# Output stores of a tiled einsum on two DMA queues, each issued behind the copies of the next tile

## Chip, cores and metric

One core of one Trainium2 chip. The metric is the device time of one launch in microseconds (us), lower is better.

## The reference

```python
def setup_inputs():
    batch, n_heads, seq_t, seq_s, channels = 8, 12, 512, 512, 64
    # x, y: (8, 12, 512, 64) float32

def reference(x, y):
    return np.einsum('bhtc,bhsc->bhts', x, y).astype(np.float32)
```

Two inputs of 12.6 MB each, one output of 100.7 MB: per head a 512 x 64 by 64 x 512 product. There is little arithmetic per byte written.

## The kernel before

The inputs are loaded in 12 groups of 8 heads (x and y, 1 MB each), cast to bf16 and rearranged, then transposed on VectorE. The output is made in 48 tiles of 128 partitions x 4096 float32 (2 MB): eight matmuls into PSUM, two copies of 1536 columns by ScalarE, one of 1024 by VectorE, and one store. Inputs and output tiles share five slots of 2 MB in SBUF.

```python
    SLOTS = 5
    # ... (views, constants cut)
    slots = ctx.enter_context(tc.tile_pool(name="slots", bufs=SLOTS))
    # ... (other pools cut)
    def slot():
        return slots.tile([P, K * S], fp32, name="slot")

    def load(g):
        both = slot()
        nc.sync.dma_start(both[:, :R * C], xv[g])
        nc.sync.dma_start(both[:, R * C:], yv[g])
        loaded[g] = both
    # ... (compress, mix, transposes cut: the input work)
    def result(o):

        i, h = divmod(o, 2)
        xT, yT = made[i]
        otf = slot()
        ot = otf.rearrange("p (r s) -> p r s", s=S)
        for k, n in ((0, 3), (3, 3), (6, 2)):
            pm = (pm3pool if n == 3 else pm2pool).tile([P, n, S], fp32, name=f"pm{n}")
            for j in range(n):
                nc.tensor.matmul(
                    pm[:, j, :], xT[:, k + j, h, :], yT[:, h * S:(h + 1) * S], start=True, stop=True
                )
            copy(nc.scalar if n == 3 else nc.vector, ot[:, k:k + n, :], pm)
        if h == 0 and i + 2 < 2 * NG:
            transposes(i + 2)
        elif h == 1 and FIRST <= i + 4 < 2 * NG:
            mix(i + 4, behind)
        return lambda: nc.sync.dma_start(ov[i, h], otf)

    with tc.manual_schedule():
        for g in range(SLOTS):
            load(g)
        # ... (memsets cut)
        stores = []
        for g in range(NG):
            compress(g)
            mix(g // 2, [nc.gpsimd] * 4, (g % 2,))
            if g in (2, 4):
                transposes(g // 2 - 1)
            if g < 5:
                load(g + SLOTS)
            elif g in (5, 7, 9):
                stores.append(result(len(stores)))
            elif g in (6, 8):
                load(g // 2 + 7)
        for store in stores:
            store()
        for o in range(len(stores), 4 * NG):
            result(o)()
```

The schedule is by hand: each engine executes its instructions in the order in which the program emits them.

Of the kernel before, what the change touches and what calls it, by code (L numbers as in the profile page):

```python
# [1 line left out]

# [4 lines left out]


@with_exitstack
def kernel(  # L10
    ctx: ExitStack,
    tc: tile.TileContext,
    x: bass.AP,
    y: bass.AP,
    out: bass.AP,
):










    nc = tc.nc
    B, H, T, C = x.shape
    _, _, S, _ = y.shape
    P = 128  # L30
    G = 8
    Q = P // G
    R = T // Q
    NG = B * H // G
    K = 8
    E = R // K
    D = 32
    SLOTS = 5
    fp32 = mybir.dt.float32
    bf16 = mybir.dt.bfloat16  # L40
    u32 = mybir.dt.uint32
    COPY = mybir.ActivationFunctionType.Copy
    assert C == 2 * D and S == T and R == D and Q * 2 == D

    xv = x.rearrange("b h t c -> (b h t c)").rearrange("(g p n) -> g p n", p=P, n=R * C)
    yv = y.rearrange("b h t c -> (b h t c)").rearrange("(g p n) -> g p n", p=P, n=R * C)
    ov = out.rearrange("b h t s -> (b h t s)").rearrange(
        "(o u h q n) -> o h q u n", u=2, h=2, q=Q * E, n=K * S
    )

    const = ctx.enter_context(tc.tile_pool(name="const", bufs=1))
    kept = ctx.enter_context(tc.tile_pool(name="kept", bufs=NG))
    slots = ctx.enter_context(tc.tile_pool(name="slots", bufs=SLOTS))
    tpool = ctx.enter_context(tc.tile_pool(name="tpool", bufs=3))
    pm3pool = ctx.enter_context(tc.tile_pool(name="pm3psum", bufs=2, space=bass.MemoryType.PSUM))
    pm2pool = ctx.enter_context(tc.tile_pool(name="pm2psum", bufs=1, space=bass.MemoryType.PSUM))

    loaded, inputs, mixed, made = {}, {}, {}, {}
    zeroed = [const.tile([P, K * E * D], u32, name=f"xb{half}") for half in range(2)]
    in_front = [nc.vector, nc.gpsimd, nc.vector, nc.scalar]  # L60
    behind = [nc.vector, nc.gpsimd, nc.scalar, nc.vector]
    FIRST = NG // 2

    def copy(engine, dst, src):
        if engine is nc.scalar:
            nc.scalar.activation(dst, src, COPY)  # L66
        else:
            engine.tensor_copy(dst, src)  # L68
# [10 lines that stand above are left out]
    def compress(g):  # L79

        both = loaded.pop(g)
        xk = kept.tile([P, R, C], bf16)
        nc.scalar.activation(xk.rearrange("p r c -> p (r c)"), both[:, :R * C], COPY)  # L83
        inputs[g] = xk
        ys = both[:, R * C:].rearrange("p (r c) -> p r c", c=C)
        for half in range(2):
            yb = kept.tile([P, R // 2 * D], u32, name=f"yb{half}")
            yv2 = yb.bitcast(bf16).rearrange("p (j c w) -> p j w c", j=R // 2, w=2)
            for ch in range(2):
                copy(  # L90
                    in_front[2 * half + ch],
                    yv2[ch * 64:(ch + 1) * 64],
                    ys[half * 64:(half + 1) * 64, :, ch * D:(ch + 1) * D].rearrange(
                        "p (j w) c -> p j w c", w=2
                    ),
                )
            mixed[2 * g + half] = yb

    def mix(i, engines, halves=(0, 1)):

        g, half = divmod(i, 2)
        xk = inputs[g]
        xv2 = zeroed[half].bitcast(bf16).rearrange("p (k e c u) -> p k e c u", k=K, e=E, u=2)
        for ch in halves:
            for u in range(2):
                lo = half * 64 + u * D
                copy(
                    engines[2 * ch + u],
                    xv2[(2 * ch + u) * D:(2 * ch + u + 1) * D, :, :, :, u],
                    xk[lo:lo + D, :, ch * D:(ch + 1) * D].rearrange("p (e k) c -> p k e c", k=K),  # L110
                )

    def transposes(i):
        xb, yb = zeroed[i % 2], mixed.pop(i)
        xT = tpool.tile([P, K * D * E], u32)
        nc.vector.transpose(  # L116
            xT.rearrange("p (k r e) -> p k e r", k=K, e=E),
            xb.rearrange("p (k e c) -> p k e c", k=K, e=E),
        )
        yT = tpool.tile([P, D * R // 2], u32)  # L120
        nc.vector.transpose(  # L121
            yT.rearrange("p (r j) -> p j r", r=D), yb.rearrange("p (j c) -> p j c", c=D)
        )
        made[i] = (xT.bitcast(bf16).rearrange("p (k h m) -> p k h m", k=K, h=2), yT.bitcast(bf16))
# [15 lines that stand above are left out]
            transposes(i + 2)  # L140
        elif h == 1 and FIRST <= i + 4 < 2 * NG:
            mix(i + 4, behind)
        return lambda: nc.sync.dma_start(ov[i, h], otf)  # L143

    with tc.manual_schedule():
        for g in range(SLOTS):
            load(g)
        nc.vector.memset(zeroed[0], 0.0)  # L148
        nc.gpsimd.memset(zeroed[1], 0.0)  # L149
# [9 lines that stand above are left out]
                stores.append(result(len(stores)))  # L159
            elif g in (6, 8):  # L160
                load(g // 2 + 7)
        for store in stores:
            store()
        for o in range(len(stores), 4 * NG):
            result(o)()


# [1 line left out]
_INS = ['x', 'y']  # L169
_OUTS = [((8, 12, 512, 512), 'float32')]  # L170


# [23 lines left out]
```

## Time and profile before

| | before |
|---|---|
| time, median of the first 3 runs | 301.96 us (301.9 to 302.25) |
| span of the profiled run | 300.5 us |
| DMA engines, share of the span | 98.7% on one queue |
| busiest compute engine | ScalarE, 66% |
| moved | 125.83 MB (read 25.17, written 100.66) |
| one store, issue to landing, median | 21.7 us |

The lines of the profile are shown in the prediction below. In a line of a stretch, the columns are the stretch, its length, busy time and instructions of PE, PEld (weight loads), DVE (VectorE), ACT (ScalarE) and POOL, then the granted TensorE clock, the mean busy share of the 16 DMA engines, and GB/s. A packet is counted in the stretch in which it starts, so a share can come out a little over 1. A packet is one entry of the trace's DMA table: in the kernel before 6144 of 16 KB (one row of a store's tile), 3072 of 8 KB (one row of a load) and 1152 of 4 bytes. Ring is used here as another word for queue. In a line of waits they are who waited, for what, us in all, times, and the longest.

### The profile page before, as it was taken

How to read it: one execution, taken by the hardware profiler on the slowest of the kernel's cores; microseconds unless marked ns; L12 is line 12 of the kernel's file. 1: busy time of each engine (PE TensorE's matmuls, PEld its weight loads, DVE VectorE, ACT ScalarE, POOL GpSimd, SP SyncE). 2: the span in 40 equal slices, each digit the busy share in tenths (PEclk: the TensorE clock that was granted, in tenths of full speed). 3: DMA queues.
4: the chain of work that ended last, by engine and by line, in shares of the span. 5: the costliest groups of instructions: out<-in, count | busy, mean ns of one | idle time of the engine just before them, and what ended most of it. 6: DMA issues, size and time to landing. Idle time of an engine off the chain costs nothing.

```text
span 300.5 us, 1448 instructions
## 1 busy us (share of the span) xinstructions
PE 148.4 (49%) x384; PEld 47.6 (16%) x384; DVE 189.2 (63%) x157; ACT 198.1 (66%) x139; POOL 82.0 (27%) x59
## 2 busy tenths in 40 slices
PE   0004044228647573765675567666476767475000
PEld 0001011003212121221121122212121222121000
DVE  1568998895997669666767576757765775313000
ACT  4666598999976867686668676777677664647000
POOL 1899989991211011101110111011101100000000
PEclk9999575577997659567756855756955765955555
DMA  7999999999999999999999999999999999999994
GB/s 282 429 424 421 423 422 422 423 435 434 423 434 426 425 438 430 425 443 421 433 436 425 432 430 425 438 430 423 442 423 430 441 421 430 432 422 427 436 425 181
DMA packets 10377, 125.93 MB, mean 419 GB/s; under 512 B 1152, under 2 KB 1152, under 8 KB 1152
## 3 DMA queue, kind: packets, MB, share of 16 engines
q1 hardware_dynamic: 10368, 125.83, 98.7%
q8 instruction: 3, 0.05, 0.1%
q14 instruction: 6, 0.05, 0.0%
HBM read 25.17 MB, written 100.66 MB: 419 GB/s over the span
## 4 chain that ended last, share of the span: by engine, by line
DMA 65%; ACT 15%; DVE 7%; PE 3%; issue 1%; ACTq 1%; SPq 0%; DVEq 0%
DMA out_dram<-slot 56%; ACT slot L66 11%; DMA slot<-in_y_dram 9%; DVE yb L68 4%; PE pm L135 3%; ACT xk L83 3%; DVE xT L116 2%; ACT yb L66 2%; DVE slot L68 1%; DVE yT L121 1%; ACTq L191 0%; SPq L75 0%; ACTq L66 0%; DVEq L68 0%; SPq L143 0%
## 5 line engine op out<-in xcount | busy, mean ns | idle before, releaser
L135 PE MATMUL pm<-yT,xT 128*128 128x512 bf16 x384 | 148.4, 537 | 127.3 <-ACT slot L66 102.2
L66 ACT ACTIVATE slot<-pm 128x1536 f32<-128x1536 f32 x96 | 133.9, 1448 | 65.8 <-DMA out_dram<-slot 51.3
L68 DVE COPY slot<-pm 128x1024 f32<-128x1024 f32 x48 | 58.8, 1225 | 72.0 <-PE pm L135 54.4
L68 POOL COPY xb<-xk 32x1024 bf16<-32x1024 bf16 x42 | 62.2, 1482 | 145.4 <-DVE xT L116 144.3
L135 PEld LDWEIGHTS <-xT 128*128 128x128 bf16 x384 | 47.6, 124 | 227.2 <-issue 193.9
L116 DVE STREAM_TRANSPOSE xT<-xb 128x1024 uint32<-128x1024 uint32 x24 | 49.3, 2054 | 0.7
L68 DVE CAST yb<-slot 64x1024 bf16<-64x1024 f32 x24 | 35.2, 1466 | 13.5 <-DMA slot<-in_y_dram 13.2
L83 ACT ACTIVATE xk<-slot 128x2048 bf16<-128x2048 f32 x12 | 22.9, 1910 | 9.6 <-DMA slot<-in_x_dram 9.4
L68 DVE COPY xb<-xk 32x1024 bf16<-32x1024 bf16 x36 | 26.3, 731 | 0.5
L121 DVE STREAM_TRANSPOSE yT<-yb 128x512 uint32<-128x512 uint32 x24 | 25.0, 1041 | 0.0
L66 ACT ACTIVATE xb<-xk 32x1024 bf16<-32x1024 bf16 x18 | 24.1, 1338 | 0.4
L68 POOL CAST yb<-slot 64x1024 bf16<-64x1024 f32 x12 | 18.8, 1567 | 8.1 <-DMA slot<-in_y_dram 7.4
L66 ACT ACTIVATE yb<-slot 64x1024 bf16<-64x1024 f32 x12 | 15.9, 1324 | 3.6 <-DMA slot<-in_y_dram 3.4
L83 ACT ACT_TABLE_LOAD x1 | 1.3, 1283 | 0.7 <-PEq L180 0.7
L148 DVE MEMSET xb<- 128x1024 uint32 x1 | 0.9, 912 | 1.0 <-PEq L180 1.0
L149 POOL MEMSET xb<- 128x1024 uint32 x1 | 1.0, 952 | 0.3 <-POOLq L180 0.3
L180 POOL MEMSET const-float32-0.0<- 128x1 f32 x1 | 0.1, 98 | 0.2 <-issue 0.2
L180 POOL MEMSET const-float32-1.0<- 128x1 f32 x1 | 0.1, 98 | 0.0
L180 POOL MEMSET const-bfloat16-1.0<- 128x1 bf16 x1 | 0.1, 98 | 0.0
L180 POOL MEMSET const-uint8-127<- 128x1 uint8 x1 | 0.1, 98 | 0.0
## 6 DMA issues: line engine op xcount, KB each, us to landing
out_dram<-slot SPq DMA_DIRECT2D x48, 2048.0 KB, 21.7
slot<-in_x_dram SPq DMA_DIRECT2D x12, 1024.0 KB, 17.5
slot<-in_y_dram SPq DMA_DIRECT2D x12, 1024.0 KB, 19.3
```

Source lines behind the costliest of these rows:

```text
L66: nc.scalar.activation(dst, src, COPY)
L68: engine.tensor_copy(dst, src)
L83: nc.scalar.activation(xk.rearrange("p r c -> p (r c)"), both[:, :R * C], COPY)
L116: nc.vector.transpose(xT.rearrange("p (k r e) -> p k e r", k=K, e=E), xb.rearrange("p (k e c) -> p k e c", k=K, e=E),)
L121: nc.vector.transpose(yT.rearrange("p (r j) -> p j r", r=D), yb.rearrange("p (j c) -> p j c", c=D))
L135: nc.tensor.matmul(pm[:, j, :], xT[:, k + j, h, :], yT[:, h * S:(h + 1) * S], start=True, stop=True)
L148: nc.vector.memset(zeroed[0], 0.0)
L149: nc.gpsimd.memset(zeroed[1], 0.0)
L180: nc = _bacc.Bacc("TRN2", target_bir_lowering=False, num_devices=1)
```

## The change

Half of the stores move to ScalarE's DMA queue, and each store is emitted only after the copies of the next tile. The intent is to have two queues feeding the DMA engines, without making ScalarE wait for VectorE's share of a tile before it may start on the next: by the time ScalarE comes to a store, the tile has long been complete.

```diff
-        return lambda: nc.sync.dma_start(ov[i, h], otf)
+        return lambda: (nc.scalar if h else nc.sync).dma_start(ov[i, h], otf)
...
-        for store in stores:
-            store()
-        for o in range(len(stores), 4 * NG):
-            result(o)()
+        done = len(stores)
+        while len(stores) > 1:
+            stores.pop(0)()
+        for o in range(done, 4 * NG):
+            stores.append(result(o))
+            stores.pop(0)()
+        stores.pop()()
```

## The prediction

A mark in a recorded text stands for a passage that is cut because no trace or run of this case shows it. In the prediction these are rules on how queues share the DMA engines, a ceiling for the rate with what rival B would gain by it in full, and a reason for rival C. The sum came to 301.9 us: the terms that stand give 302.0, and a term of -0.1 us is cut. The lower end of the range, 299.5 us, and "B nearly whole" rested on a cut ceiling for the rate, which wasn't shown.

> **What bounds the kernel now.** I read the page first: the share of each engine, the slices, then the queues.
>
> ```profile
> PE 148.4 (49%) x384; PEld 47.6 (16%) x384; DVE 189.2 (63%) x157; ACT 198.1 (66%) x139; POOL 82.0 (27%) x59
> ...
> DMA  7999999999999999999999999999999999999994
> GB/s 282 429 424 421 423 422 422 423 435 434 423 434 426 425 438 430 425 443 421 433 436 425 432 430 425 438 430 423 442 423 430 441 421 430 432 422 427 436 425 181
> ...
> q1 hardware_dynamic: 10368, 125.83, 98.7%
> HBM read 25.17 MB, written 100.66 MB: 419 GB/s over the span
> ```
>
> No compute engine is busy for more than 66% of the span. The 16 DMA engines are busy for 98.7% of it on the one queue in use, and every slice but the first and the last is full. So the time is 125.83 MB at the rate at which the engines take packets, plus the two ends: 1.3% of 300.5 us is 3.9 us for start and tail together. Next I asked for stretches, in case one hides a hole.
>
> ```profile
> 0.00:54.10 54.10, 10.44 (x24) 3.37 (x25) 38.93 (x29) 36.84 (x24) 44.69 (x33) 0.82 0.98 404
> 54.10:66.00 11.90, 3.61 (x8) 1.09 (x8) 10.71 (x8) 11.67 (x9) 11.10 (x8) 0.64 1.03 432
> 66.00:72.60 6.60, 5.13 (x14) 1.80 (x14) 3.59 (x4) 5.96 (x5) 2.33 (x2) 0.56 1.01 432
> 72.60:278.30 205.70, 129.23 (x339) 41.30 (x337) 135.96 (x119) 143.64 (x104) 23.85 (x18) 0.69 1.01 430
> 278.30:295.00 16.70, 0.00 (x0) 0.00 (x0) 0.00 (x0) 0.00 (x0) 0.00 (x0) 0.50 1.00 428
> 295.00:300.50 5.50, 0.00 (x0) 0.00 (x0) 0.00 (x0) 0.00 (x0) 0.00 (x0) 0.50 0.21 89
> ```
>
> The last two columns are the DMA engines' share and GB/s. The share is 1 from the first few microseconds to 295; a hole that stores issued in another way could fill isn't there. In the last 16.7 us nothing computes: the stores already issued drain, at the same rate. Third, the waits and the chain.
>
> ```profile
> ACT slot L66 <- DMA out_dram<-slot: 51.3, 33, 2.7
> ACT slot L66 <- PE pm L135: 10.8, 8, 2.3
> ```
>
> ```profile
> 253.62 21.71 DMA out_dram<-slot
> 275.33 0.02 issue
> 275.35 0.04 ACTq L66
> 275.39 0.04 issue
> 275.44 1.45 ACT slot L66
> ```
>
> ScalarE waits for stores to land and free one of the five slots, not the stores for ScalarE. A store lands 21.7 us after its issue (the median in the page's list of DMA issues too), while 2.097 MB take 2.097/0.430 = 4.9 us of all engines. So it stands behind 21.7/4.9 = 4.4 tiles of work: the queue is deep, and its depth is only what five slots allow.
>
> [...] The trace before has one store's issue at 538 to 653 ns on SyncE, 48 of them 26 us of an otherwise idle queue, so there is little to save. [...]
>
> **The change part by part.**
>
> First, 24 of 48 stores (the h = 1 ones, odd tiles) move to ScalarE. SyncE loses 24 x 0.54 = 13 us that nobody waited for, ScalarE gains 13 us: 198.1 + 13 = 211 us in 300, 70%. In steady state a pair of tiles lasts 2 x 4.9 = 9.8 us. ScalarE has four copies at 1.45, in most pairs one 1.34 us mix, and now 0.54: 7.7 us. It fits, and what is lost comes out of the wait for landing (45.4 us of those 51.3 lie between 130 and 277 us). On the path: nothing.
>
> Second, each store is placed behind the next tile's copies. For even tiles on SyncE this means nothing: its queue holds no copies, and it goes on as soon as ScalarE and VectorE have written the tile. For odd tiles it does: the built order on ScalarE is copies of tile n, then the store of tile n-1. And the copies of tile n first wait for the store of tile n-5 to land, since it has their slot. So a finished odd tile lies idle until the next slot is free and two copies are done.
>
> How far does this drain the queue? Call a the moment at which odd store n-5 lands. Tile n is copied by about a + 3 us (two 1.45 us copies), and then n-1 goes out on ScalarE and n on SyncE, nearly together. Each queue gets one 2.1 MB store per 9.8 us at the same moment, and if they share equally the two land nearly together. At a, then, only n-3 and n-2 are still in flight, with up to 4.2 MB or 9.8 us of work; at a + 3 there are 6.8 us left. Before, a new store found about 21.7 - 4.9 = 16.8 us ahead of it. The queue loses more than half of its depth, but does not run dry. Time from issue to landing: two pairs, 19.6 us, less the 3 us of copying, so some 16.5 us where the pairs land together, up to 21.4 for SyncE's if the queues stay half a cycle apart. I expect the median at 16 to 20.
>
> Third, the start, the thinnest place. Store 1 was issued at about 54.7 us and now stands behind ScalarE's input work up to 65.9. By 66 the engines have moved 54.1 x 404 + 11.9 x 432 = 27.0 MB; issued are 25.17 of loads plus stores 0 and 2 (4.19): 29.36 MB, so 2.4 MB or 5.5 us are left when store 1 joins. Store 3 moves from 68.8 to after tile 4's copies, some 72.4. By then 2.85 MB more have gone and 2.10 come: 1.6 MB or 3.7 us left, against 3.7 MB before. Still no hole. Tile 3 starts 0.5 us later, hidden.
>
> Fourth, the end. The last store is still issued as soon as its tile is copied, and all bytes drain at the full rate; if one queue is empty first, the other has the engines alone, as the single queue has now. Tail: unchanged, within a few tenths.
>
> Sum: 302.0 + 0 (issue) + 0 (later odd stores) + 0 (start) +/- 0.3 (end). [...]
>
> **Rivals.**
>
> A, the queue runs dry. ScalarE's queue is held up in its program order, and one late copy keeps two tiles from going out. For it: the depth falls from 16.8 to some 6.8 us, 3.7 at the start. Against it: copies need only 3 us, and the tail shows that the engines differ by just some 3 us in when they finish (share 0.21 over the last 5.5 us), less than 6.8; besides, a fast engine that idles costs nothing while the slowest has work. If each of the 24 pairs left a hole of 0.3 us, the time would be 302 + 24 x 0.3 = 309 us: slower by 2.4%.
>
> B, two rings are faster for the packets: while one finishes a store, the other has data. For it: 125.83 MB in 98.7% of 300.5 us is 424 GB/s[...]. Against it: the share is already 1.0, with four stores queued in one ring the next packet always stands ready. [...]
>
> C, alternating between two stores makes the packets slower[...]. The trace has one mixed stretch, 54 to 66 us, loads and stores queued together, at 432 GB/s: no sign. One per cent would make 305.
>
> **Range and chances.** The bound, bytes through engines that are always fed, isn't touched; I expect 301.9 us. B in part gives the lower end, C or a few small holes the upper: 299.5 to 304.5. More than 2% either way needs 6 us: B nearly whole (2 to 3%), or A in earnest (3 to 4%).
>
> **What would show it.** Right: two queues of about 50 and 75 MB in the list, each near its share of bytes, and together within half a per cent of 98.7%; every slice of DMA at 9 from the second to the last but one; median landing 16 to 20 us; ScalarE at 69 to 71% with its DMA issues counted in (the page doesn't count them, so its busy time stays at 198); more ScalarE waits that end with a landing, in pairs. Wrong: slices of 7 or 8 in the steady part (A), a rate of 433 or more over 130 to 270 us (B) or of 426 or less there at a full share (C), or a tail after 295 us that is longer than 5.5 us by a microsecond or more.

## The result and the profile after

| | before | after |
|---|---|---|
| time, median | 302.11 us (4 runs) | 302.34 us (4 runs) |
| DMA share, by queue | 98.7% | 59.5% + 39.3% |
| waits of ScalarE's output copies for a landing | 51.3 us, 33 times | 59.4 us, 21 times |
| waits of VectorE's output copies for a landing | 15.8 us, 9 times | 45.6 us, 20 times |
| last store issued at | 278.3 us | 281.0 us |

The ratio is 1.0002, 95% interval 0.9987 to 1.0017: the same. A ratio here is the mean time of one kernel's fast runs over that of the other's fast runs of the same rounds, so it isn't quite the ratio of the medians quoted.

The page of the changed kernel: DMA share and rate in 40 slices, and the queues.

```profile
DMA  7999999999999999999999999999999999999994
GB/s 285 436 419 419 420 427 427 420 430 439 424 433 432 424 437 430 424 443 424 426 445 421 426 439 424 428 441 424 428 440 422 433 432 426 417 432 439 421 424 201
...
q1 hardware_dynamic: 6912, 75.50, 59.5%
q10 hardware_dynamic: 3456, 50.33, 39.3%
```

The first line is digit for digit that of the kernel before: full from the second slice to the last but one. The bytes have split over two queues, 75.5 and 50.3 MB, and the shares add up to 98.8% in place of 98.7%.

The stretches of the changed kernel that answer to those of the prediction:

```profile
54.10:66.00 11.90, 3.63 (x8) 1.11 (x8) 10.74 (x8) 11.67 (x9) 11.12 (x8) 0.56 1.02 427
66.00:72.60 6.60, 5.32 (x13) 1.83 (x13) 3.56 (x4) 5.73 (x5) 2.12 (x2) 0.50 1.02 437
...
130.00:230.00 100.00, 58.37 (x163) 20.53 (x166) 68.70 (x62) 71.21 (x52) 14.43 (x11) 0.76 1.01 431
...
278.30:295.00 16.70, 1.28 (x4) 0.15 (x1) 1.22 (x1) 1.92 (x2) 0.00 (x0) 0.50 1.00 426
295.00:300.20 5.20, 0.00 (x0) 0.00 (x0) 0.00 (x0) 0.00 (x0) 0.00 (x0) 0.50 0.22 91
```

No hole at the start, 431 GB/s in the middle, and a tail of the same shape. For the middle, the same stretch of the kernel before:

```profile
130.00:230.00 100.00, 64.50 (x163) 20.50 (x162) 67.88 (x60) 70.06 (x51) 13.26 (x10) 0.65 1.01 431
```

What did move lies ahead of the DMA engines. Waits, then DMA issues (KB each, median us to landing), of the changed kernel:

```profile
ACT slot L67 <- DMA out_dram<-slot: 59.4, 21, 4.1
ACT slot L67 <- PE pm L136: 4.4, 21, 0.5
```

```profile
out_dram<-slot SPq DMA_DIRECT2D x24, 2048.0 KB, 18.0
out_dram<-slot ACTq DMA_DIRECT2D x24, 2048.0 KB, 19.5
```

Fewer and longer waits: the slots now come free in pairs, one store on each queue landing nearly together (the last completions of such a pair at 155.52 and 156.72 us, of the next at 165.31 and 166.55), so ScalarE waits once for two tiles. The timeline of the changed kernel shows the place where a store is issued on ScalarE's queue (start, duration, engine):

```profile
155.60 1.45 ACT L67 ACTIVATE slot<-pm 128x1536 f32<-128x1536 f32 x1 [2.60 <-DMA out_dram<-slot]
...
155.71 0.55 ACTq L144 DMA_DIRECT2D out_dram<-slot  x1
...
156.95 2.79 ACT L67 ACTIVATE slot<-pm 128x1536 f32<-128x1536 f32 x2
```

In program order the store stands behind two copies of the even tile. It is issued 0.11 us after the first of them has begun, while that copy runs, and the next starts at 156.95, as the first one ends (155.60 + 1.45 = 157.05; back-to-back copies overlap a little). The issue took nothing from the copies.

### The profile page after: what moved, and what is told of

Its sections match the earlier page's. It is cut to its first block, busy times and chain, and to the rows that moved or that the text cites. A ratio compares the mean times of both kernels' runs of the same rounds, so it can differ in the third digit from the quotient of the medians.

```text
span 300.2 us, 1437 instructions
## 1 busy us (share of the span) xinstructions
PE 137.7 (46%) x377; PEld 47.7 (16%) x384; DVE 189.5 (63%) x157; ACT 198.5 (66%) x139; POOL 82.1 (27%) x59
## 3 DMA queue, kind: packets, MB, share of 16 engines
q1 hardware_dynamic: 6912, 75.50, 59.5%
q10 hardware_dynamic: 3456, 50.33, 39.3%
## 4 chain that ended last, share of the span: by engine, by line
DMA 79%; DVE 6%; ACT 6%; PE 1%; issue 1%; SPq 0%; ACTq 0%; DVEq 0%
DMA out_dram<-slot 70%; DMA slot<-in_y_dram 9%; DVE yb L69 4%; ACT slot L67 3%; ACT xk L84 2%; DVE xT L117 1%; ACT yb L67 1%; PE pm L136 1%; DVE slot L69 1%; DVE yT L122 1%; SPq L76 0%; ACTq L67 0%; DVEq L69 0%
## 5 line engine op out<-in xcount | busy, mean ns | idle before, releaser
L136 PE MATMUL pm<-yT,xT 128*128 128x512 bf16 x377 | 137.7, 525 | 141.9 <-ACT slot L67 117.0
L67 ACT ACTIVATE slot<-pm 128x1536 f32<-128x1536 f32 x96 | 134.2, 1449 | 67.5 <-DMA out_dram<-slot 59.4
L69 DVE COPY slot<-pm 128x1024 f32<-128x1024 f32 x48 | 58.8, 1225 | 75.8 <-DMA out_dram<-slot 45.6
L69 DVE CAST yb<-slot 64x1024 bf16<-64x1024 f32 x24 | 35.2, 1465 | 13.4 <-DMA slot<-in_y_dram 13.1
## 6 DMA issues: line engine op xcount, KB each, us to landing
out_dram<-slot ACTq DMA_DIRECT2D x24, 2048.0 KB, 19.5
slot<-in_y_dram SPq DMA_DIRECT2D x12, 1024.0 KB, 19.2
```

The costliest lines, as they stand in the source:

```text
L67: nc.scalar.activation(dst, src, COPY)
L69: engine.tensor_copy(dst, src)
L136: nc.tensor.matmul(pm[:, j, :], xT[:, k + j, h, :], yT[:, h * S:(h + 1) * S], start=True, stop=True)
```

## The experiments

Two theories. **Fed engines**: the time is bytes through DMA engines that always have work; the queue and the moment of issue don't matter until the work in flight runs out. **Cancelling effects**: two rings move packets faster, the later issue loses it again. Each experiment's edit is against the changed kernel. One that suggests itself, all stores on SyncE behind the next tile's copies, isn't there: the order of instructions and waits on every engine is that of the kernel before, since SyncE's queue has no copies for a store to stand behind.

### Two queues, no delay

```diff
-        while len(stores) > 1:
+        while len(stores) > 0:
             stores.pop(0)()
         for o in range(done, 4 * NG):
             stores.append(result(o))
             stores.pop(0)()
-        stores.pop()()
```

> The two queues alone: each store is issued straight after its own tile's copies. Theory (the 16 DMA engines are always fed, so neither the queue nor the moment of issue matters): within 0.5% of the kernel before, 301 to 303.5 us, DMA share 98 to 99%; landing of ScalarE's stores after 19 to 21 us, as they are issued sooner. Rival (the change is two opposite effects that cancel: two rings move packets faster, the late issue loses it again): faster than before by over 1%, under 299 us, with more than 433 GB/s in the steady part.

Measured: 302.27 us against 302.30, ratio 1.0000 (0.9988 to 1.0013); 431 GB/s between 130 and 230 us. Its DMA issues:

```profile
out_dram<-slot SPq DMA_DIRECT2D x24, 2048.0 KB, 18.0
out_dram<-slot ACTq DMA_DIRECT2D x24, 2048.0 KB, 23.0
```

ScalarE's stores are issued 3.5 us earlier relative to their landing (23.0 against 19.5, more than the 21 expected) and the time doesn't change. The second queue alone gains nothing, and the delay added to it takes nothing, so nothing cancels.

### All stores on ScalarE, behind one and behind three further tiles

```diff
-        return lambda: (nc.scalar if h else nc.sync).dma_start(ov[i, h], otf)
+        return lambda: nc.scalar.dma_start(ov[i, h], otf)
...
-        while len(stores) > 1:
+        while len(stores) > LAG:              # 1; 3; 4; 0
             stores.pop(0)()
         for o in range(done, 4 * NG):
             stores.append(result(o))
-            stores.pop(0)()
-        stores.pop()()
+            if len(stores) > LAG:
+                stores.pop(0)()
+        while stores:
+            stores.pop(0)()
```

> All 48 stores on ScalarE's queue, each behind the copies of the next tile; SyncE has loads only. Theory: the queue holds three to four stores, never runs dry, 301 to 303.5 us. Median landing 19.5 us = 4 x 4.87, as a store goes out when the slot of the tile four places before it has landed. Rival (cancelling effects): the late issue without a second ring is slower by over 1%, over 305 us.

> As one_queue_lag1, but each store behind the copies of the third tile after it. While ScalarE waits for a landing only one store is left in flight. Theory: 4.9 us of work must cover the time from a landing over the issue (0.55 us) to the first packet (some 2 us at the start of the trace before) and the 3.6 us by which the slowest engine trails; the time is set by the slowest engine, which still has work, so 302 to 306 us; landing after about 9.7 us (2 x 4.87). Rival (depth matters from the first step): a steady loss with each step of lag, 3% or more here.

Measured: 304.38 us with LAG = 1, ratio 1.0069 (1.0055 to 1.0083), and 306.72 us with LAG = 3, ratio 1.0149 (1.0135 to 1.0163). Both are outside what the theory expected; the median landing is not (19.2 and 9.6 us). The "some 2 us" to the first packet were too much: in the trace before it starts at 1.76 us, 1.0 us after the first issue has begun (0.74). The stretches of LAG = 1, then of LAG = 3:

```profile
54.10:66.00 11.90, 3.46 (x8) 1.11 (x8) 10.71 (x8) 11.67 (x9) 11.09 (x8) 0.64 0.84 351
66.00:72.60 6.60, 5.16 (x15) 1.83 (x15) 3.57 (x4) 6.11 (x5) 2.28 (x2) 0.59 1.00 425
...
130.00:230.00 100.00, 62.27 (x159) 20.24 (x162) 69.47 (x62) 71.10 (x52) 13.51 (x11) 0.68 1.01 427
```

```profile
54.10:66.00 11.90, 3.63 (x8) 1.11 (x8) 10.71 (x8) 11.67 (x9) 11.09 (x8) 0.68 0.76 317
66.00:72.60 6.60, 5.27 (x14) 1.83 (x14) 3.56 (x4) 5.78 (x5) 2.17 (x2) 0.54 0.76 320
```

The share has a hole here and nowhere later. It is the start: the finished stores 0 to 2 stand in ScalarE's program behind its work on the inputs, the first goes out at 62.80 us (LAG = 1) or 63.67 us (LAG = 3) in place of 54.14, and the loads have run out by then. The hole is (1 - 0.84) x 11.9 = 1.9 us with LAG = 1, and (1 - 0.76) x (11.9 + 6.6) = 4.4 us with LAG = 3; the times are longer by 2.1 and 4.4 us (what sets the time is the slowest engine and not this mean, so the match is rougher than it looks; see "The first three stores on SyncE"). But 427 GB/s in the middle, in place of 431, left a second reading of the first of these: packets that move more slowly from ScalarE's queue. The run that tells them apart follows after the next two.

### Behind the fourth tile

> Behind the copies of the fourth tile after it: ScalarE waits for the only store in flight before it issues the next. Theory: now the queue does run dry once per tile, and each of about 44 tiles leaves a hole of 2 to 3 us: 390 to 440 us, DMA share about 70%, landing 7 to 8 us. Rival (the issue is not what feeds the engines): under 320 us.

Measured: 395.21 us, ratio 1.3077. From its timeline (the waits that two of the copies ended on stand in brackets), and a stretch:

```profile
207.66 1.45 ACT L67 ACTIVATE slot<-pm 128x1536 f32<-128x1536 f32 x1 [2.65 <-DMA out_dram<-slot]
...
207.71 0.55 ACTq L144 DMA_DIRECT2D out_dram<-slot  x1
...
214.51 0.55 ACTq L144 DMA_DIRECT2D out_dram<-slot  x1
```

```profile
130.00:230.00 100.00, 51.41 (x113) 15.67 (x114) 48.81 (x45) 49.78 (x36) 10.00 (x8) 0.50 0.72 303
```

Now each store waits for the landing of the one before, 6.7 us after its issue (7 to 8 were expected). A tile takes 214.51 - 207.71 = 6.80 us in place of 4.87 (2.097 MB at 430 GB/s). So for 1.93 us the engines have nothing to move, between the last bytes of one store and the first of the next, and the share falls to 0.72 = 4.87/6.80. Times 44 tiles the 1.93 us are 85 of the 93 us; most of the rest is a longer hole at the start (share 0.66 from 54.1 to 66 us and 0.45 from there to 77). The rival of this run, that issue isn't what feeds the engines, falls. This is where the order of stores begins to matter: with one store left in flight the engines are fed, with none they aren't.

### Behind their own copies

LAG = 0: ScalarE's sequencer stops at each store until VectorE has finished the tile.

> All stores on ScalarE's queue, each right behind its own copies, so ScalarE's sequencer waits for the last copies of the tile, VectorE's too, before it goes on to the next tile: the stall that the change's order avoids. Theory: the stall (1 to 2 us per tile) is taken out of ScalarE's wait for landings, 301 to 304 us. Rival (the order behind the next tile's copies is what keeps the second queue harmless): over 306 us.

Measured: 304.39 us, ratio 1.0072 (1.0057 to 1.0087), the same as with LAG = 1, with the same hole at the start (share 0.83 from 54.1 to 66), and just over the 304 us expected. The stall that the change's order is made to avoid costs nothing here beyond that hole: the times of LAG = 0 and 1 are 304.39 and 304.38 us. That it comes out of ScalarE's waits for landings was the author's estimate and isn't shown: they are 56.9 us here and 56.5 with LAG = 1.

### The first three stores on SyncE

```diff
-        return lambda: (nc.scalar if h else nc.sync).dma_start(ov[i, h], otf)
+        return lambda: (nc.sync if o < 3 else nc.scalar).dma_start(ov[i, h], otf)
...
-        while len(stores) > 1:
+        while stores:
             stores.pop(0)()
         for o in range(done, 4 * NG):
             stores.append(result(o))
-            stores.pop(0)()
-        stores.pop()()
+            if len(stores) > LAG:             # 1; 3
+                stores.pop(0)()
+        while stores:
+            stores.pop(0)()
```

> As one_queue_lag1, but stores 0, 1 and 2 go out on SyncE as in the kernel before, so that they don't stand behind ScalarE's work on the inputs; the other 45 stay on ScalarE, each behind the next tile's copies. Theory: the 2.1 us of one_queue_lag1 come from the hole at 54 to 66 us (DMA share 0.84 there): now no hole, share 1.0 there, 301.5 to 302.8 us. Rival (packets move more slowly on ScalarE's queue: 427 GB/s at full share between 130 and 230 us in one_queue_lag1, 431 in the kernel before): 304 us or more, still 427.

Measured: 301.73 us against 302.25, ratio 0.9985 (0.9973 to 0.9998).

```profile
54.10:66.00 11.90, 3.63 (x8) 1.10 (x8) 10.74 (x8) 11.67 (x9) 11.12 (x8) 1.00 1.03 434
...
130.00:230.00 100.00, 61.71 (x160) 20.23 (x163) 68.05 (x60) 70.38 (x51) 13.21 (x10) 0.69 1.01 432
```

The hole is gone, and with it the whole loss, though 45 of 48 stores still go through ScalarE's queue; and the rate is 432 GB/s there too. So that queue isn't slow, and the start is what one_queue_lag1 lost. Why the rate in the middle was 427 in the runs with a hole isn't shown, but the traces show that it cost nothing. The packed trace keeps 16 completion times for each store. From the tenth store to the 47th, the mean of the 16 comes every 4.91 or 4.92 us in each of the four profiles with a single hole (LAG = 0, 1 and 3 above, and the next run), and every 4.88 in the kernel before and in this version. The last of the 16, which sets the time, comes every 4.90 us with a hole, and every 4.93 and 4.91 in these two: no later. In the kernel before, the last trails the first by 1.5 us at the tenth store and by 3.5 at the end, with a hole by 1.5 to 1.7 at the end. So GB/s, a mean of all engines, isn't the pace of the slowest.

The version is also 0.15% faster than the kernel before; the interval excludes 1 only just, and no cause for it was looked for.

> As one_queue_lag3, with stores 0, 1 and 2 on SyncE at once. Theory: the 4.4 us of one_queue_lag3 were the hole between 54 and 72.6 us (share 0.76), not the single store left in flight later: 301.5 to 303 us. Rival (one store in flight costs something in every tile): 304 to 307 us.

Measured: 303.18 us, ratio 1.0034 (1.0021 to 1.0047): 3.5 of the 4.4 us are back, not all, and the time is just past the expected upper end. Two stretches of it:

```profile
75.00:82.50 7.50, 4.66 (x18) 1.73 (x18) 7.42 (x8) 7.43 (x7) 2.19 (x2) 1.00 0.85 358
...
130.00:230.00 100.00, 60.50 (x160) 19.83 (x163) 69.54 (x63) 71.06 (x53) 13.20 (x10) 0.70 1.00 426
```

The rest is one more hole, (1 - 0.85) x 7.5 = 1.1 us, at a place where ScalarE and VectorE are busy for 7.4 of 7.5 us: the copies behind which the stores stand are themselves catching up with the input work. Later the share is 1.00 with one store in flight, and the last of a store's 16 completions comes every 4.90 us, so that costs nothing per tile, though the mean rate is 426.

### Half of the bytes

To see what the bytes are worth, each store writes the first half of each row only. Once in the kernel before, once in the changed one. Their outputs are wrong, which doesn't matter for the times.

```diff
-        return lambda: (nc.scalar if h else nc.sync).dma_start(ov[i, h], otf)
+        return lambda: (nc.scalar if h else nc.sync).dma_start(ov[i, h][:, :, :K * S // 2], otf[:, :K * S // 2])
```

> The kernel before, but each store writes only the first half of each row of its tile (8 KB of 16), so the result is wrong on purpose: 75.5 MB in place of 125.8. Theory: bytes are the bound, so the time falls, to what the compute engines need after the loads: DMA alone would be 75.5/0.430 = 176 + 4 us; ScalarE has 198 us of work; I expect 215 to 240 us with the DMA share at 73 to 83%. Rival (something other than bytes paces the stores, such as issue or landing): over 270 us.

> The changed kernel with the same half stores (wrong on purpose), to see what the change does where DMA is not the bound. If ScalarE is then the bound and an issue takes its time, 24 x 0.55 = 13 us or less are lost against half_bytes_before (up to 6% slower); if ScalarE's sequencer issues beside the running copy, as the trace after shows it (issue 0.1 us after the first copy's start), under 1.5% either way.

Measured: 222.48 and 222.70 us, both 0.7364 of the kernel before. ScalarE's slices and a piece of the timeline, of the changed kernel with half stores:

```profile
ACT  2666665989998999999999999999999999999990
```

```profile
158.06 1.34 ACT L67 ACTIVATE xb<-xk 32x1024 bf16<-32x1024 bf16 x1
158.94 0.55 ACTq L144 DMA_DIRECT2D out_dram<-slot  x1
...
159.42 2.79 ACT L67 ACTIVATE slot<-pm 128x1536 f32<-128x1536 f32 x2
```

Both are as expected. Bytes were the bound, since there are as many stores and rows as before: 50.3 MB fewer take 79.7 us off, until ScalarE is full. And with ScalarE full, 24 issues of 0.55 us would be 13 us, or 6%, if they took its time; the difference of the medians is 0.2 us. The copy at 159.42 starts when the one before ends, whatever was issued between.

### Each store cut in two over both queues

By partitions (64 each), then by columns (128 partitions, half of each row):

```diff
-        return lambda: (nc.scalar if h else nc.sync).dma_start(ov[i, h], otf)
+        def both():
+            for part, engine in enumerate((nc.sync, nc.scalar)):
+                engine.dma_start(
+                    ov[i, h][part * 32:(part + 1) * 32], otf[part * 64:(part + 1) * 64]
+                )
+        return both
```

```diff
+            n = K * S // 2
+                    ov[i, h][:, :, part * n:(part + 1) * n], otf[:, part * n:(part + 1) * n]
```

> Each tile's store cut in two by partitions, one half on each queue, behind the next tile's copies on ScalarE: both rings always work at the same tile. Theory: 301 to 303.5 us, DMA share 98 to 99%. If alternating between rings cost or saved time per packet it would show here too[...].

Measured: 371.73 to 380.9 us, ratio 1.2356 (1.229 to 1.2421); the runs scatter, so two of the four, the profiled one too, are counted as slow; the ratio is of the other two. The expectation failed by far. From its trace:

```profile
130.00:230.00 100.00, 52.10 (x120) 16.34 (x122) 51.88 (x47) 54.40 (x40) 9.28 (x7) 0.63 1.00 321
```

The engines are busy all the time and move a quarter less: a full share is not a full rate. Either the 64 partitions of each transfer or the second queue within a tile may be the cause, and two further runs were to tell which.

> The store cut in two as in two_queues_halves, but by columns: each queue takes all 128 partitions and half of each row (8 KB). Theory: [...] 301 to 304 us, share 98 to 99%. Rival[...]: over 330 us.

> The store cut in two by partitions (64 each), both halves on SyncE, so no second ring. Theory[...]: as slow as two_queues_halves or slower[...]: 370 to 530 us. Rival (the second ring was the cause): 301 to 304 us.

Measured by columns on two queues: 304.41 us, just over the expected 304, ratio 1.0076 (1.0061 to 1.0091), 422 GB/s from 130 to 230 us at share 1.01. So two queues within one tile aren't what costs a quarter. The 0.8% may come from rows of 8 KB in place of 16 (loads, also of 8 KB rows, run at 425 in the kernel before); that isn't shown. Measured by partitions on one queue (halves_one_queue, the diff with `(nc.sync, nc.sync)`): 312.10 us, ratio 1.0329, far less than expected.

```profile
66.00:72.60 6.60, 5.12 (x12) 1.72 (x12) 3.55 (x4) 5.73 (x5) 2.33 (x2) 0.50 1.02 238
...
130.00:230.00 100.00, 63.36 (x159) 20.19 (x161) 67.88 (x60) 69.44 (x51) 13.24 (x10) 0.65 1.01 426
```

At first it runs at 238 GB/s, then it recovers to 426. The 16 completion times drift apart meanwhile: the last of a half-store trails the first by 0.4 us at the first one, by 4.7 at the sixth and by 5.7 to 7.2 from 110 us on, over two half-stores of 2.44 us (1.05 MB at 430 GB/s). Whether this is why the rate recovers isn't shown. On two queues the loss stays for the whole run, with SyncE's halves completing within 2.3 to 4.8 us and ScalarE's over 13.4 to 15.8 us (those issued from 137 to 346 us). Neither the cut by partitions (3.3% on one queue) nor the second queue (0.8% by columns) explains it alone; why it stays with two is open. It doesn't touch the change, whose stores have all 128 partitions each.

## Why the prediction was right

- **The bound.** Right, and shown from both sides: the share is the same to 0.1 points, and taking bytes away took 79.7 us off.
- **Issue cost, the first part.** The result, nothing on the path, was right; the size wasn't. ScalarE does not lose 13 us, not even when it is full (half_bytes_after): its sequencer issues while a copy runs (at 155.71 us, in the copy from 155.60 to 157.05). Counted in, the issues would make it busy for 70%, as predicted, but that time isn't taken from anything.
- **Depth of the queue, the second part.** The pairs, the sharing of the two rings (between 130 and 230 us 1320 packets of 16 KB from SyncE's queue and 1310 from ScalarE's) and the median (18.0 and 19.5 us, predicted 16 to 20) came as predicted. The term "Call a the moment ... by about a + 3 us ... then n-1 goes out on ScalarE" was mis-sized by almost 3 us for ScalarE's store: it goes out 0.1 us after the first copy has begun (155.71 against 155.60 us), not after both. So it is in flight for two pairs (19.5 us), not 16.5. The error lay on the safe side: the queue is fuller than worked out. SyncE's 18.0 lies between the two cases given. "More ScalarE waits" was half right: they come in pairs and last longer in all (59.4 us against 51.3), but are fewer (21 against 33).
- **The start.** It was called the thinnest place, rightly: each single-queue run with stores 0 to 2 behind the input work lost time there. In the change stores 0 and 2 still go out early on SyncE (54.0 and 59.2 us), and the share is 1.02. Store 1 was issued at 62.6 us, not 65.9, and store 3 at 70.2, not 72.4, for the same reason as above.
- **The end.** The last store is issued 2.7 us later and the tail after 295 us is as long as before (5.2 and 5.5 us). One queue is empty first, and the other has the engines alone: from 294 to 296 us all packets are from ScalarE's queue, 0.85 MB, which is 426 GB/s.
- **The rivals.** A takes losing the last store in flight (one_queue_lag4), or a queue held up at the start. B falls: 431 GB/s with one ring or two. C falls: 431 at full share, and a 16 KB packet takes 612 ns between 130 and 230 us in both kernels, on either queue.

## What to carry to other kernels

When the DMA engines are full from end to end, don't expect a gain from more queues or another order of issue: here neither moved the time by 2% as long as one store was left in flight (1.0149 at most). Fewer bytes did (0.7364), and so did losing that last store in flight (1.3077), or cutting stores by partitions (1.0329 on one queue, 1.2356 on two). Before a store moves to a compute engine's queue, look at what stands ahead of it in that engine's program, at the start above all: 2.1 and 4.4 us were lost there. Read GB/s beside the DMA share, since engines can be fully busy at three quarters of the rate (two_queues_halves: 321 GB/s at a share of 1.00, 431 in the kernel before).
